# ConvFFN of layer 1 of a diffusion backbone: six up-projection tiles ahead of the norm, H in tiles of its own, eight PSUM banks in turn

## The chip, the cores and the metric

The kernel runs on one core of one Trainium2 chip. The metric is the device time of one execution in microseconds (us). TensorE multiplies matrices into PSUM (eight banks of 512 fp32 columns), ScalarE and VectorE work on SBUF and PSUM, GpSimd on SBUF, and SyncE issues the loads.

## The reference, cut to what matters

Two layers act on 256 latent tokens (and 256 context tokens, which the last layer no longer updates). Behind the token mixer each layer has a gated ConvFFN with a modulated norm in front of it:

```python
def _conv_ffn(h, P):
    u = h @ P['w_up']                                    # 1024 -> 5632
    up = jnp.pad(u, ((0, 0), (1, 1), (0, 0)))
    cw = P['conv_w']
    u = up[:, :-2] * cw[0] + up[:, 1:-1] * cw[1] + up[:, 2:] * cw[2] + P['conv_b']
    g, val = jnp.split(u, 2, axis=-1)
    return (jax.nn.silu(g) * val) @ P['w_down']          # 2816 -> 1024
...
    xl = xl + g1 * y_l
    xl = xl + g2 * _conv_ffn(_rmsnorm(xl, P['norm_ffn']) * (1 + sc2) + sh2, P)
```

All is fp32.

## The kernel before

Features lie on the partitions and tokens on the columns. In layer 1 a tile has 128 features of the 256 latent tokens. To keep fp32's accuracy each product is three matmuls (`mm3`, lines 172 to 174): high part of the weights by high part of the activations, high by low, low by high. `load_w` brings 512 columns of weights (256 KB) into a slot of a ring, lets ScalarE round the high part (line 164) and VectorE or GpSimd subtract the low part (line 168). `lo_on_pool(a, b)` sends a of every b low parts to GpSimd. In the ConvFFN of layer 1 the rings have eight slots in all, so weights can be ready up to four up tiles ahead of TensorE. `unit` makes one output tile of two loads: 8 blocks of rows x 3 matmuls = 24 matmuls.

The ConvFFN has 44 up tiles (called units 0 to 43 here), taken in pairs: `inner(f)` takes units 2f and 2f + 1, lets `conv` apply the three-point convolution to each (ScalarE line 1139, VectorE lines 1142 and 1143), multiplies with the gate (ScalarE 1171, VectorE 1172 and 1173) and splits the product into `ach` (ScalarE 1176) and `acl` (VectorE 1177). These 22 inner tiles are multiplied with the down weights in three groups, of tiles 0 to 7, 8 to 15 and 16 to 21, each with eight output tiles that are added to x (line 1197). The first group comes after inner tile 8, the second and the third after inner tile 21.

In front of it stands the norm: sums of squares on TensorE (line 233), a chain of small VectorE operations that makes the factor (`rsqrt`, lines 197 to 207, and `dg`, line 239), a matmul that spreads it over the partitions (line 242), a copy of it (line 279), and eight steps `hmod`, each of which makes one block of the normed input H: VectorE 265, ScalarE 266, VectorE 267. TensorE does not wait for it in layer 1: while the norm runs, units 0 to 3 are computed ahead from x scaled per feature, which stands in columns 256 to 511 of the `xeh`/`xel` tiles (two columns in front hold the shift, so 258 columns are taken). The factor and the shift are applied to the products afterwards, in `up` (VectorE 1131 and 1132, ScalarE 1133). `run(hsteps, k, UP4)` hands out the norm's ten steps between the blocks k of these units: the sums behind block 1, the spreading behind block 4, the `hmod` steps behind blocks 5 to 7. H is then written into columns 0 to 255 of the same tiles, over the two shift columns, so it follows the reads of units 0 to 3.

The products go to PSUM banks: units 0 to 3 to the four banks of two pair tiles "s" and "t", all later ones in turn to two banks "m" and two banks "o" (`bank`), each of which must have been read by `conv` before it is written again.

The program is written in the order above, and a planner sets each engine's order from it: within an engine it may take a later instruction first when an earlier one isn't ready by its reckoning.

Of the kernel before, what the change touches and what calls it, by code (L numbers as in the profile page):

```python
# [6 lines left out]
F32 = mybir.dt.float32  # L7
F32R = mybir.dt.float32r
# [9 lines left out]
KT = 8  # L18
T = 256
# [13 lines left out]
def hybrid(nc, tc, I, out, dbg=None, stop=None):  # L33
    dbg = dbg or {}
    es = ExitStack()
    mm = nc.tensor.matmul
# [13 lines left out]
    def psum(tag, w=512):  # L50
        return ps.tile([128, 512], F32, tag=tag, name="ps_" + tag, bufs=2)[:, :w]
# [95 lines left out]
    def lo_on_pool(a, b, c=0):  # L147

        lo_mix[:] = [a, b, c]
# [3 lines left out]
    def open_ring(st, name, n):  # L153

        rings.append((st.enter_context(pool(name)), n))
        st.callback(rings.pop)
# [14 lines left out]
    def mm3(o, ah, al, bh, bl, start, stop):  # L171
        mm(o, ah, bh, start=start, stop=False)  # L172
        mm(o, ah, bl, start=False, stop=False)  # L173
        mm(o, al, bh, start=False, stop=stop)  # L174

    def unit(ap, ah, al, w, nk=8, c0=0, p=None, pre=None):
        p = psum("mm", w) if p is None else p
        for k0 in range(0, nk, 4):
            n = min(4, nk - k0)
            hi, lo = pre.pop(0) if pre else load_w(ap[:, 128 * k0:128 * (k0 + n)], 128 * n)  # L180
            for kk in range(n):
                k = k0 + kk
                c = slice(kk * 128, kk * 128 + 128)
                mm3(p, hi[:, c], lo[:, c], ah[k][:, c0:c0 + w], al[k][:, c0:c0 + w], k == 0, k == nk - 1)
        return p
# [98 lines left out]
    def run(steps, i, plan):  # L284

        for _ in range(plan.get(i, 0)):
            if steps:
                steps.pop(0)()


    UNITS = {0: 1, 2: 1, 3: 2, 4: 2, 5: 2, 6: 2}
    UP4 = {1: 1, 4: 1, 5: 3, 6: 3, 7: 2}
    FIRST = {0: 1, 2: 1, 3: 2, 4: 2, 5: 2, 6: 2}
    carried = []

# [21 lines left out]
    def layer(l):  # L317
# [777 lines left out]
        with pool(f"f{l}") as fp, ExitStack() as rst:  # L1095
            nf = (3, 2)[l]
            ps_s, ps_t = pair2("s"), pair2("t")
            p4 = [ps_s[:, 0], ps_s[:, 1], ps_t[:, 0], ps_t[:, 1]]
            for s in range(NS):
                q = slice(T * s, T * s + T)  # L1100
                for k in range(KT):
                    wh, wl = load_w(I["wup4"][l, k], 512)
                    for u in range(4):
                        c = slice(128 * u, 128 * u + 128)
                        if last:
                            mm3(p4[u][:, :T + 2], wh[:, c], wl[:, c], Hh[k][:, T - 2:], Hl[k][:, T - 2:], k == 0, k == KT - 1)
                        else:
                            mm3(p4[u][:, q], wh[:, c], wl[:, c], Hh[k][:, q], Hl[k][:, q], k == 0, k == KT - 1)
                    run(hsteps, k, UP4)
                while hsteps:  # L1110
                    hsteps.pop(0)()
                if s == 0:
                    open_ring(rst, f"ringf{l}", nf)

            lo_on_pool(*((1, 1), (1, 3))[l])

            turn = [0]

            def bank(w):
                turn[0] += 1  # L1120
                t = ("mmst", "mmoo")[l][turn[0] % 4]
                return psum("mm", w) if t == "m" else psum("o", w) if t == "o" else pair2(t)[:, 0, :w]

            def up(i):
                if i >= 4:
                    return unit(I["wup"][l, i], Hh, Hl, W, p=bank(W))
                if not last:
                    return p4[i]
                u = fp.tile([128, T], F32, tag="ue", name="ue", bufs=2)
                cu = small.tile([128, 1], F32, tag="cu", name="cu")  # L1130
                V.tensor_copy(cu, p4[i][:, 0:1])
                V.tensor_tensor(out=u, in0=p4[i][:, 2:T + 2], in1=rb, op=ALU.mult)
                S.activation(u, u, AF.Identity, bias=cu)
                return u

            def conv(p, t):
                y = fp.tile([128, NTOK], F32, tag="cy", name="cy", bufs=4)[:, :W]
                w = [P(l, O_CONVW + 44 * i + t) for i in range(3)]
                S.activation(y, p, AF.Identity, bias=P(l, O_CONVB + t), scale=w[1])
                pv = p.rearrange("p (s t) -> p s t", t=T)  # L1140
                yv = y.rearrange("p (s t) -> p s t", t=T)
                V.scalar_tensor_tensor(out=yv[:, :, 1:], in0=pv[:, :, :T - 1], scalar=w[0], in1=yv[:, :, 1:], op0=ALU.mult, op1=ALU.add)
                V.scalar_tensor_tensor(out=yv[:, :, :T - 1], in0=pv[:, :, 1:], scalar=w[2], in1=yv[:, :, :T - 1], op0=ALU.mult, op1=ALU.add)  # L1143
                return y

            mtodo = {}
            if not last:
                def later(key, l, tiles, both=True):
                    mtodo.setdefault(key, []).extend([lambda t=t: modcol(fp, l, t, both) for t in tiles])
                for i in range(4):  # L1150
                    later(3 + i, 0, range(40 + 2 * i, 42 + 2 * i))
                mtodo[6].append(lambda: modsum(0, 5))
                for j in range(8):
                    later((0, j), 1, [j])
                    later(8 + j, 1, [8 + j])
                    later((1, j), 1, range(16 + 2 * j, 18 + 2 * j), False)
                mtodo[15].append(lambda: (modsum(1, 0), modsum(1, 1), ab(1, 0)))
                for i in range(5):
                    later(16 + i, 1, range(32 + 3 * i, 35 + 3 * i), False)
                later(19, 1, [47], False)  # L1160
                mtodo.setdefault((2, 4), []).append(lambda: ([modsum(1, wh, 1) for wh in (2, 3, 4, 5)], ab(1, 1, False)))

            def todo(key, ins):
                with tc.issue_after(ins):
                    for g in mtodo.pop(key, []):
                        g()
            def inner(f):
                g = conv(up(2 * f), f)
                v = conv(up(2 * f + 1), FT + f)
                th = fp.tile([128, NTOK], F32, tag="th", name="th", bufs=2)[:, :W]  # L1170
                S.activation(th, g, AF.Tanh, scale=0.5)  # L1171
                V.scalar_tensor_tensor(out=g, in0=th, scalar=1.0, in1=g, op0=ALU.add, op1=ALU.mult)
                V.tensor_tensor(out=v, in0=g, in1=v, op=ALU.mult)
                hi = fp.tile([128, W], F32R, tag="ach", name="ach", bufs=nac)
                lo = fp.tile([128, W], F32R, tag="acl", name="acl", bufs=nac)
                S.activation(hi, v, AF.Copy, scale=0.5)  # L1176
                r = V.scalar_tensor_tensor(out=lo, in0=v, scalar=0.5, in1=hi.bitcast(F32), op0=ALU.mult, op1=ALU.subtract)
                todo(f, r.ins)
                ach.append(hi)
                acl.append(lo)  # L1180


            groups = ([[0, 8, 10], [8, 16, 18], [16, 22, 22]], [[0, 8, 9], [8, 16, 22], [16, 22, 22]])[l]
            nac = (11, 22)[l]
            ach, acl = [], []
            for gi, (f0, f1, done) in enumerate(groups):
                while len(ach) < done:
                    inner(len(ach))
                end = gi == len(groups) - 1
                if end and not last:  # L1190
                    lo_on_pool(0, 1)
                for ss in ([[s] for s in range(NS)] if end else [list(range(NS))]):
                    for j in range(KT):
                        p = unit(I["wdn"][l, j][:, 128 * f0:128 * f1], ach[f0:f1], acl[f0:f1], T * len(ss), nk=f1 - f0, c0=T * ss[0], p=bank(T * len(ss)))
                        for i, s in enumerate(ss):
                            c = slice(T * s, T * s + T)
                            r = V.scalar_tensor_tensor(out=x[j][:, c], in0=p[:, T * i:T * i + T], scalar=mcol(l, 5, s, j), in1=x[j][:, c], op0=ALU.mult, op1=ALU.add)
                        todo((gi, j), r.ins)
                        run(hsteps, j, UNITS)
                    if end and not last:  # L1200
                        while hsteps:
                            hsteps.pop(0)()
                        hsteps = norm(1, 0, ss[0])
            carried[:] = hsteps if not last else []
# [143 lines left out]
```

## Time and profile before

| | us |
|---|---|
| median of three runs | 1488.95 (1488.82 to 1491.21) |
| profiled execution, time | 1488.52 |
| its span in the profile | 1486.7 |
| TensorE busy | 1421.6 (96%) |
| VectorE busy | 1205.5 (81%) |
| ScalarE busy | 808.8 (54%) |
| GpSimd busy | 430.5 (29%) |

Times in the rows are microseconds from the span's start. PE is TensorE's matmuls, DVE VectorE, ACT ScalarE, POOL GpSimd. The ConvFFN of layer 1 runs from about 1279 to 1475. Matmuls overlap in the pipeline: the time from one start to the next is their pace, and the duration shown is longer. Some matmul records can be missing. PEclk is the granted clock of TensorE as a share of 2.4 GHz.

### The profile page before, as it was taken

To read this page: it belongs to the slowest core of one execution; us is meant where nothing else is said; L and a number is where in the kernel's file an instruction comes from. 1 tells how busy PE (TensorE), PEld (TensorE's weight loads), DVE (VectorE), ACT (ScalarE), POOL (GpSimd) and SP (SyncE) were. 2 spreads that over 40 slices of the span, in tenths; PEclk is the share of its full clock that TensorE was granted. 3 is DMA by queue.
4 is the path that set the end of the run, shared out by engine and by line. 5 is a ranking of instruction groups with operands and counts; after the bars stand their busy time and mean duration, and the time that the engine had idled before them with its cause. 6 is when DMAs were issued, how large, how long until landed. Compare 5 with 4: busy or idle time off the path is not lost.

```text
span 1486.7 us, 28000 instructions
## 1 busy us (share of the span) xinstructions
PE 1421.6 (96%) x10222; PEld 1241.3 (83%) x10222; DVE 1205.5 (81%) x2316; ACT 808.8 (54%) x1690; POOL 430.5 (29%) x325
## 2 busy tenths in 40 slices
PE   6999989999999999999999999998899899989997
PEld 4787867778788899888888889997788789989997
DVE  4689797878886788898878979979677876997885
ACT  3575455656653356533344235675467666665663
POOL 0001333233320002547544630002244442223331
PEclk9999999999999999999999999999899999999998
DMA  8522132232335576454655865532223336556563
GB/s 312 171 84 67 43 99 90 79 92 89 100 117 176 154 227 207 128 165 144 206 149 160 296 223 149 184 126 69 82 83 94 95 114 191 176 162 198 175 173 92
DMA packets 108650, 213.45 MB, mean 144 GB/s; under 512 B 12128, under 2 KB 21728, under 8 KB 107488
## 3 DMA queue, kind: packets, MB, share of 16 engines
q1 hardware_dynamic: 107824, 211.00, 45.9%
q8 instruction: 81, 1.33, 0.4%
q10 hardware_dynamic: 688, 0.66, 0.1%
q14 instruction: 57, 0.47, 0.1%
HBM read 210.56 MB, written 1.05 MB: 142 GB/s over the span
## 4 chain that ended last, share of the span: by engine, by line
PE 79%; DVE 15%; ACT 3%; issue 3%; DMA 1%; SPq 0%; DVEq 0%; ACTq 0%
PE ps_mm L172 15%; PE ps_mm L174 15%; PE ps_mm L173 15%; PE ps_pair L172 5%; PE ps_pair L174 5%; PE ps_pair L173 5%; PE ps_o L174 2%; PE ps_o L172 2%; PE ps_o L173 2%; PE ps_pair L867 2%; PE ps_pair L905 2%; DVE wlo L168 1%; PE ps_o L924 1%; PE ps_o L921 1%; DVE p L889 1%
## 5 line engine op out<-in xcount | busy, mean ns | idle before, releaser
L168 POOL TENSOR_TENSOR wlo<-raw,whi 128x512 fp32r<-128x512 f32 (+1 forms) x270 | 378.0, 1405 | 833.3 <-ACT whi L164 573.5
L164 ACT CAST whi<-raw 128x512 fp32r<-128x512 f32 (+1 forms) x614 | 360.6, 597 | 301.9 <-PE ps_mm L173 125.5
L172 PE MATMUL ps_mm<-hh,whi 128*128 128x512 f32 (+1 forms) x760 | 275.3, 362 | 3.3 <-DVE qf L997 2.0
L173 PE MATMUL ps_mm<-hl,whi 128*128 128x512 f32 (+1 forms) x760 | 271.8, 358 | 0.0
L174 PE MATMUL ps_mm<-hh,wlo 128*128 128x512 f32 (+1 forms) x760 | 271.1, 357 | 0.0
L168 DVE TENSOR_TENSOR wlo<-raw,whi 128x512 fp32r<-128x512 f32 (+1 forms) x344 | 233.5, 689 | 34.8 <-ACT whi L164 31.8
L172 PEld LDWEIGHTS ps_mm<-hh,whi 128*128 128x128 f32 x760 | 144.5, 190 | 27.4 <-issue 3.2
L174 PEld LDWEIGHTS ps_mm<-hh,wlo 128*128 128x128 f32 x760 | 144.3, 190 | 22.5 <-issue 0.4
L173 PEld LDWEIGHTS ps_mm<-hl,whi 128*128 128x128 f32 x760 | 144.5, 190 | 21.0 <-issue 0.4
L104 DVE SCALAR_TENSOR_TENSOR jk<-wm,sil 128x1024 f32<-128x1024 f32 x96 | 153.3, 1597 | 1.6 <-DMA wm<-wmod 0.6
L172 PE MATMUL ps_pair<-hh,whi 128*128 128x512 f32 (+1 forms) x312 | 109.7, 353 | 0.6 <-ACT whi L164 0.6
L174 PE MATMUL ps_pair<-hh,wlo 128*128 128x512 f32 (+1 forms) x312 | 109.0, 352 | 0.3 <-DVE wlo L168 0.2
L173 PE MATMUL ps_pair<-hl,whi 128*128 128x512 f32 (+1 forms) x312 | 109.2, 351 | 0.0
L909 ACT CAST pth<-ps_pair 128x512 fp32r<-128x512 f32 (+1 forms) x96 | 49.5, 516 | 46.1 <-PE ps_pair L905 29.4
L172 PEld LDWEIGHTS ps_pair<-hh,whi 128*128 128x128 f32 x312 | 58.5, 188 | 9.9 <-ACT whi L164 1.2
L174 PEld LDWEIGHTS ps_pair<-hh,wlo 128*128 128x128 f32 x312 | 58.4, 188 | 9.7 <-DVE wlo L168 0.9
L910 DVE TENSOR_TENSOR ptl<-ps_pair,pth 128x512 fp32r<-128x512 f32 (+1 forms) x96 | 57.3, 597 | 11.0 <-ACT pth L909 10.2
L173 PEld LDWEIGHTS ps_pair<-hl,whi 128*128 128x128 f32 x312 | 58.6, 188 | 8.6
L172 PE MATMUL ps_mm<-ach,whi 128*128 128x256 f32 (+1 forms) x200 | 63.7, 319 | 1.6 <-ACT ach L1176 1.1
L173 PE MATMUL ps_mm<-acl,whi 128*128 128x256 f32 (+1 forms) x200 | 63.5, 317 | 0.0
L174 PE MATMUL ps_mm<-ach,wlo 128*128 128x256 f32 (+1 forms) x200 | 63.4, 317 | 0.0
L1171 ACT ACTIVATE th<-cy 128x512 f32<-128x512 f32 (+1 forms) x44 | 23.0, 523 | 59.8 <-DVE cy L1143 59.6
(684 smaller groups left out, 3687.7 us busy)
## 6 DMA issues: line engine op xcount, KB each, us to landing
raw<-wup SPq DMA_DIRECT2D x184, 256.0 KB, 3.2
raw<-win SPq DMA_DIRECT2D x166, 256.0 KB, 2.8
wm<-wmod SPq DMA_DIRECT2D x64, 512.0 KB, 4.2
raw<-wdn SPq DMA_DIRECT2D x88, 256.0 KB, 3.0
raw<-wbr SPq DMA_DIRECT2D x48, 256.0 KB, 2.7
raw<-wout SPq DMA_DIRECT2D x48, 256.0 KB, 3.0
wm<-wm SPq DMA_DIRECT2D x8, 1024.0 KB, 8.3
wm<-wmod SPq DMA_DIRECT2D x32, 256.0 KB, 2.6
```

The costliest lines, as they stand in the source:

```text
L104: V.scalar_tensor_tensor(out=jk, in0=wm, scalar=1.0, in1=sil[:, s], op0=ALU.mult, op1=ALU.mult, accum_out=MOD[l][:, s, t:t + 1])
L164: S.copy(hi[:, :ncols], raw[:, :ncols])
L168: e.tensor_tensor(out=lo[:, :ncols], in0=raw[:, :ncols], in1=hi[:, :ncols].bitcast(F32), op=ALU.subtract)
L172: mm(o, ah, bh, start=start, stop=False)
L173: mm(o, ah, bl, start=False, stop=False)
L174: mm(o, al, bh, start=False, stop=stop)
L867: mm(sp[:, i, :w], q[:, qc], k[:, kc], start=a == 0, stop=a == n - 1 and not mk)
L889: (G if i < (0, 1)[l] else V).tensor_scalar(out=pts[1 - i], in0=pts[1 - i], scalar1=st_[:, 7 - i:8 - i], scalar2=None, op0=ALU.mult)
L905: nc.tensor.transpose(tp[:, i, c], pts[i][:, c], ident)
L909: S.copy(dh, tv)
L910: V.tensor_tensor(out=dl, in0=tv, in1=dh.bitcast(F32), op=ALU.subtract)
L1171: S.activation(th, g, AF.Tanh, scale=0.5)
```

## The change

Everything is in layer 1's ConvFFN, except that the weight ring is opened one statement earlier in both layers.

- Units 4 and 5 are also computed ahead from the scaled x, into the two banks "m". The norm's spreading step stands behind block 6 in place of 4, three `hmod` steps behind block 7, four behind unit 4 and one behind unit 5.
- H gets sixteen tiles of its own, 256 columns wide (`fhh`, `fhl`).
- The factor and the shift are applied to all six tiles at once, before the first inner tile, into six buffers.
- All later tiles take eight banks in turn: o, o, both halves of s, both halves of t, m, m.
- The low parts of the weights are made on VectorE alone (before: one of three on GpSimd) until inner tile 6, and one of three on GpSimd from there.

```diff
     UP4 = {1: 1, 4: 1, 5: 3, 6: 3, 7: 2}
+    UP4L = {1: 1, 6: 1, 7: 3}
...
+            xeh, xel = list(Hh), list(Hl)
+            if last:
+                for k in range(KT):
+                    Hh[k] = fp.tile([128, T], F32R, name=f"fhh{k}")
+                    Hl[k] = fp.tile([128, T], F32R, name=f"fhl{k}")
...
-                            mm3(p4[u][:, :T + 2], wh[:, c], wl[:, c], Hh[k][:, T - 2:], Hl[k][:, T - 2:], k == 0, k == KT - 1)
+                            mm3(p4[u][:, :T + 2], wh[:, c], wl[:, c], xeh[k][:, T - 2:], xel[k][:, T - 2:], k == 0, k == KT - 1)
...
-                    run(hsteps, k, UP4)
+                    run(hsteps, k, UP4L if last else UP4)
+                if s == 0:
+                    open_ring(rst, f"ringf{l}", nf)
+                if last:
+                    for i in (4, 5):
+                        p4.append(unit(I["wup"][l, i], xeh, xel, T + 2, c0=T - 2, p=psum("mm", T + 2)))
+                        run(hsteps, i, {4: 4})
                 while hsteps:
                     hsteps.pop(0)()
-                if s == 0:
-                    open_ring(rst, f"ringf{l}", nf)
-
-            lo_on_pool(*((1, 1), (1, 3))[l])
+
+            lo_on_pool(*((1, 1), (0, 1))[l])
...
+            half = {}
             def bank(w):
                 turn[0] += 1
-                t = ("mmst", "mmoo")[l][turn[0] % 4]
+                if last:
+
+                    t = "oossttmm"[(turn[0] - 1) % 8]
+                    if t in "st":
+                        if t not in half:
+                            half[t] = pair2(t)
+                            return half[t][:, 0, :w]
+                        return half.pop(t)[:, 1, :w]
+                else:
+                    t = "mmst"[turn[0] % 4]
                 return psum("mm", w) if t == "m" else psum("o", w) if t == "o" else pair2(t)[:, 0, :w]
             def up(i):
-                if i >= 4:
+                if i >= len(p4):
                     return unit(I["wup"][l, i], Hh, Hl, W, p=bank(W))
-                if not last:
-                    return p4[i]
-                u = fp.tile([128, T], F32, tag="ue", name="ue", bufs=2)
+                return p4[i] if not last else us[i]
+
+            def scaled(i):
+                u = fp.tile([128, T], F32, name=f"ue{i}")
                 cu = small.tile([128, 1], F32, tag="cu", name="cu")
                 V.tensor_copy(cu, p4[i][:, 0:1])
                 V.tensor_tensor(out=u, in0=p4[i][:, 2:T + 2], in1=rb, op=ALU.mult)
                 S.activation(u, u, AF.Identity, bias=cu)
                 return u
+            us = [scaled(i) for i in range(len(p4))] if last else []
...
                 while len(ach) < done:
+                    if last and len(ach) == 6:
+                        lo_on_pool(1, 3)
                     inner(len(ach))
```

## Rows read from the trace of the kernel before

**Rows 1.** The page, busy time, share of the span and instructions of each engine.
```profile
PE 1421.6 (96%) x10222; PEld 1241.3 (83%) x10222; DVE 1205.5 (81%) x2316; ACT 808.8 (54%) x1690; POOL 430.5 (29%) x325
```
**Rows 2.** Busy time by stretch: length, then PE, PEld, DVE, ACT, POOL, clock, DMA.
```profile
1290.00:1308.00 18.00, 15.21 (x127) 14.81 (x125) 18.00 (x43) 15.27 (x33) 7.45 (x3) 1.00 0.37 116
1308.00:1314.00 6.00, 5.72 (x36) 5.75 (x37) 4.75 (x14) 3.83 (x9) 0.00 (x0) 0.72 0.12 43
1314.00:1330.00 16.00, 15.15 (x130) 14.82 (x130) 15.97 (x28) 8.93 (x18) 6.38 (x4) 1.00 0.70 213
1330.00:1341.00 11.00, 11.00 (x98) 11.00 (x98) 9.31 (x18) 7.04 (x16) 4.39 (x3) 1.00 0.67 194
1362.00:1434.00 72.00, 71.42 (x623) 70.97 (x621) 60.67 (x111) 44.81 (x93) 22.24 (x16) 1.00 0.60 175
```
**Rows 3.** TensorE in order of time: start, duration, line, tiles; idle before, releaser.
```profile
1278.82 0.29 PE L172 MATMUL ps_pair<-xeh,whi 128*128 128x258 f32 x1
...
1282.52 0.36 PE L172 MATMUL ps_pair<-xeh,whi 128*128 128x258 f32 x1
...
1288.62 0.70 PE L242 MATMUL ps_o<-dg,ones 128*128 128x256 f32 x2 [1.55 <-DVE dg L239]
1288.97 0.47 PE L172 MATMUL ps_pair<-xeh,whi 128*128 128x258 f32 x1
...
1308.28 0.55 PE L172 MATMUL ps_mm<-xeh,whi 128*128 128x256 f32 x1 [3.07 <-ACT ach L1176]
...
1311.62 0.32 PE L172 MATMUL ps_mm<-xeh,whi 128*128 128x256 f32 x1
...
1361.68 0.29 PE L172 MATMUL ps_o<-xeh,whi 128*128 128x256 f32 x1
...
1434.49 0.36 PE L172 MATMUL ps_mm<-ach,whi 128*128 128x256 f32 x1 [0.54 <-DVE cy L1143]
```
**Rows 4.** VectorE in order of time.
```profile
1295.39 0.41 DVE L1132 TENSOR_TENSOR ue<-ps_pair,x 128x256 f32<-128x256 f32 x1
...
1298.21 0.68 DVE L168 TENSOR_TENSOR wlo<-raw,whi 128x512 fp32r<-128x512 f32 x1
1298.81 0.47 DVE L1143 SCALAR_TENSOR_TENSOR cy<-ue,pp,cy 128x255 f32<-128x255 f32 x1
1299.21 1.52 DVE L1142 SCALAR_TENSOR_TENSOR cy<-ue,pp,cy 128x255 f32<-128x255 f32 x1
...
1303.78 1.51 DVE L1143 SCALAR_TENSOR_TENSOR cy<-ue,pp,cy 128x255 f32<-128x255 f32 x1
...
1315.21 1.52 DVE L1177 SCALAR_TENSOR_TENSOR acl<-cy,ach 128x256 fp32r<-128x256 f32 x1
...
1340.65 0.42 DVE L1177 SCALAR_TENSOR_TENSOR acl<-cy,ach 128x256 fp32r<-128x256 f32 x1 [0.48 <-ACT ach L1176]
```
**Rows 5.** GpSimd in order of time.
```profile
1283.37 1.65 POOL L168 TENSOR_TENSOR wlo<-raw,whi 128x512 fp32r<-128x512 f32 x1 [35.20 <-ACT whi L164]
...
1302.83 2.18 POOL L168 TENSOR_TENSOR wlo<-raw,whi 128x512 fp32r<-128x512 f32 x1 [2.38 <-ACT whi L164]
1314.83 3.06 POOL L168 TENSOR_TENSOR wlo<-raw,whi 128x512 fp32r<-128x512 f32 x2 [9.83 <-ACT whi L164]
```
**Rows 6.** TensorE in order of time: first matmuls of runs with one moving tile.
```profile
1241.88 0.28 PE L172 MATMUL ps_mm<-ybh,whi 128*128 128x256 f32 x1
...
1243.30 0.29 PE L172 MATMUL ps_mm<-hh,whi 128*128 128x256 f32 x1
...
1369.86 0.28 PE L172 MATMUL ps_o<-xeh,whi 128*128 128x256 f32 x1
...
1375.30 0.28 PE L172 MATMUL ps_mm<-xeh,whi 128*128 128x256 f32 x1
...
1443.19 0.28 PE L172 MATMUL ps_mm<-ach,whi 128*128 128x256 f32 x1
...
1448.95 0.28 PE L172 MATMUL ps_o<-ach,whi 128*128 128x256 f32 x1
```

## The prediction

> **What bounds the kernel now.** I read the page first: TensorE is busy for 96% of the span [rows 1], so a gain must come from a stretch in which TensorE waits or runs slowly. The table by stage then shows where that is. Through most of layer 1's ConvFFN (1362 to 1434 us) TensorE is busy 71.4 of 72 us. Only the opening, 1290 to 1314, shows a hole; and there VectorE is busy 18.00 of 18 us, then 4.75 of 6, 15.97 of 16 and 9.31 of 11 [rows 2]. So in the opening two engines are near their limit, and VectorE is idle only 1.25 + 0.03 + 1.69 = 3.0 of 51 us. TensorE's list in order of time names the holes [rows 3]: 1.55 us until the norm's factor (dg) is ready, 3.07 us at 1308.28 until a PSUM bank is evacuated (the row names ach; unit 8 needs unit 4's bank, whose last reader, on VectorE, ended at about that time), and then a granted clock of 0.72 over 1308 to 1314 [rows 2], that is 1.2 GHz for part of it: sixteen matmuls from 1308.28 to 1311.62 take 3.34 us, at the later pace 1.8, so 1.5 us lost. The last wait in this stretch is therefore VectorE's, and the question is whether the change takes work from VectorE or only lets TensorE run ahead of it.
>
> **What VectorE spends.** A low part costs it 0.60 us (1298.21 to 1298.81 [rows 4]). A low part on GpSimd is not free for it: operations that take 0.47 or 0.42 us take 1.52, 1.51 and 1.52 at 1299.21, 1303.78 and 1315.21, just while GpSimd runs a low part (for example 1302.83, 2.18 us) [rows 4, 5]. Each of those held VectorE by about 1.05 us, more than the work itself.
>
> **The pace of a matmul.** With H, which lies in the left half of tiles of 512 columns, 48 matmuls of 256 columns take 1375.30 - 1369.86 = 5.44 us, 0.1133 each. With the FFN's own inner tiles as moving operand, 48 take 1448.95 - 1443.19 = 5.76, 0.1200 each; with the attention's output yb, 12 take 1.42, 0.118 each [rows 6], all at a granted clock of 1.00. Weights, ring and banks are of the same kinds, so the moving tile makes the difference; why, the rows don't tell. The change gives H tiles of its own, 256 columns wide, like every tile that shows 0.118 to 0.120. I take 0.120, and keep 0.1133 for the range.
>
> The Trainium skill (TensorE: Matmul & The Clock Gate, Back-to-back issue gap) gives the gap from the number of columns alone, N / 2.4 + 2.5 ns, 109 ns for 256; by it H's new place would cost nothing, and the sum below would end near 1486.4 in place of 1490.5. The two paces above are at odds with it.
>
> **TensorE alone, by the rows.** From the first matmul of the tiles ahead (1278.82) to the end of the first down group (1361.68) it took 82.9 us [rows 3]. After the change, with no wait: six tiles ahead, 144 matmuls of 258 columns x 0.12 = 17.3; the norm's small matmuls 0.8 + 0.35 = 1.2 (24 matmuls and the first of these fill the 3.70 from 1278.82 to 1282.52, and the second runs from 1288.62 to 1288.97); units 6 to 17, 12 x 24 x 0.12 = 34.6; eight down tiles, 8 x 24 x 0.12 = 23.0. Sum 76.1, 6.8 less. From 1361.68 to 1434.49 it took 72.8 for 26 up tiles, bank waits included (0.54 is the last, 1434.49). After: 26 x 24 x 0.12 = 74.9, 2.1 more, though eight banks take those waits away. Behind that only the inner tiles are read, at the pace of before. The two columns more of units 4 and 5 are inside the 0.12. TensorE alone would end 4.7 us earlier.
>
> **Whether VectorE lets it.** The first down tile needs the eighth inner tile. Before, its low half (acl) ran from 1340.65 to 1341.07 [rows 4]; TensorE came to it at 1361.68 - 7 x 2.88 - 3 x 0.12 = 1341.2, with 0.1 us of slack. After, TensorE by itself would be there 6.8 us earlier, at 1334.4. VectorE's sum up to that acl changes so:
> - The factor's matmul moves behind k = 6: 1282.52 + 60 x 0.12 = 1289.7 in place of 1288.6 [rows 3], so H starts 1.1 later (the 1.55 us wait itself goes). +1.1.
> - Two more scaled tiles, a copy and a product each, 0.4 together (the product 0.41, 1295.39 [rows 4]): +0.8. ScalarE gets two more Identity operations; it is busy 15.3 of 18 us there [rows 2], so I let them hide.
> - Six low parts of units 4 to 11 come from GpSimd; the first two (from 1283.37 on [rows 5]) fall into time that VectorE has to spare before the factor is due, four count: +4 x 0.60 = +2.4. The stalls that go with them go too, the three named: -3.2. One further low part can now be made before H starts: -0.6.
> - Of VectorE's idle 3.0 us, the 1.25 in 1308 to 1314 came from the slow TensorE: -1.25. The rest is ScalarE's turn within a chain, and stays.
> Net -0.75: the acl is there at about 1340.3, and TensorE, ready at 1334.4, waits 6 us somewhere before it. Bounds: -4 if all idle time is recovered and no low part comes before its turn; +2.3 if nothing is recovered and three further low parts (1.8) stand ahead.
>
> A wait of 3.07 us was followed by the 1.5 us of 1.2 GHz, the one of 1.55 was not [rows 3]. Six microseconds in one piece would cost 1.5, in small pieces nothing: I take 0.75.
>
> H's own tiles save a wait of the norm's writes for the matmuls that still read the old ones; nothing waited for that before, since the steps ran behind them: 0, and needed only because six tiles are ahead. The scaled tiles with buffers of their own: 0 by themselves. Eight banks in turn: they take a wait away only where VectorE follows in time. The loads are the same in number and size.
>
> **The sum.** Opening: -0.75 + 0.75 = 0. Units 18 to 43: +2.1. Bank waits there are inside it. The profiled execution took 1488.52 us (span 1486.7), so 1490.6, say 1490.5; the median of the runs shown, 1488.95, lies 0.4 above it, within their scatter. The change removes what TensorE waits for, not what VectorE has to do, and the gain is handed back there.
>
> **Rivals.**
> 1. *TensorE really gets ahead* (0.22). VectorE isn't held by GpSimd in the first twelve units, fills its waits, and the eighth inner tile is there by 1335.5. For it: 3.2 us of stalls do go. Against it: VectorE would have to do its 48 busy us of this stretch 5 us sooner. -4.7 + 0.7 for small waits: 1484.5.
> 2. *The pace of H does not change* (0.12). Opening 0, units 18 to 43 at 0.1133: 70.7, -2.1: 1486.4. Against it the tiles of rows 6. Both 1 and 2 (0.05): 12 x 24 x 0.0067 = 1.9 more in the opening and 4.2 more behind: 1478.
> 3. *Low parts come behind the inner chains* (0.20), the other side. In program order scaled tiles and three inner tiles now stand ahead of unit 6's weights. VectorE: H until 1290.9 + 16 x 0.4 = 1297.3, scaled 2.5, three inner tiles of seven operations, 8, to 1307.8, then unit 7's low part, 1308.4. TensorE is there at 1291.5 + 3.5 x 2.88 = 1301.6 and waits 6.8 us in one piece, then 10.5 units x 2.88 + 1.5 at the lower clock: the first down tile begins at 1340.1 against 1338.6, +1.5, and +2.1 behind. With ScalarE's casts late in the same way (up to 1.5): 1492 to 1494. It decides from a wait of about 5.5 us on with the lower clock behind it. For it: at 1308.28 TensorE waited behind the same chains.
> 4. *The turn of banks does not do what it says* (0.03): two of eight banks are halves of one pair tile. If the write of a second half waits for the first half's readers, two of eight tiles wait 1.5 us, 15 of 62: 23 us, 1512.
> The likeliest, as summed, has 0.38; its own range is 1487.5 to 1493.5.
>
> **How the numbers follow.** A measurement of this kernel can tell about 0.2%, 3 us, from no change: 1486.0 to 1491.9 is "same". Faster: rivals 1 and both, and a little of 2: 0.29. Slower: most of 3, 4, and the upper end of the likeliest: 0.27. Same: 0.44. The range goes from 1482 (rival 1 with 2.5 us to spare) to 1494.5 (rival 3's upper end); outside are 4, both of 1 and 2, and tails.
>
> **What would show it.** Right: TensorE no longer waits for dg; a wait or waits of 5 to 7 us in all before the eighth inner tile, with VectorE busy through them; no operation of VectorE of 1.5 us between 1290 and 1315; up tiles of the middle at 2.88 us each instead of 2.72; the first down tile within 1.5 us of 1338.6. Wrong: up tiles still at 2.72 (rival 2), or the first down tile before 1335 (rival 1), or one wait of over 6 us before unit 8 (rival 3).

## The result and the profile after

The changed kernel takes 1501.82 us (median of 4 runs, 1498.29 to 1503.45) beside 1490.08 for the kernel before on the same chip: a ratio of 1.0071, interval 1.0055 to 1.0087. It is 0.7% slower, about 10.6 us by the ratio and 11.7 by the medians. The forecast was 1490.5 in a range from 1482 to 1494.5; the time lies above that range.

In the profiled execution TensorE's busy time rises by 9.4 us against [rows 1], for the same 10222 matmuls; the page's line of busy time, share of the span and instructions:
```profile
PE 1431.0 (95%) x10222; PEld 1249.3 (83%) x10222; DVE 1195.8 (80%) x2325; ACT 811.3 (54%) x1692; POOL 417.0 (28%) x320
```
To say where the time went, I measure one stretch in every trace: from the first matmul that sums the squares of the norm (it stands among the tiles ahead) to the first of the final norm. Before it lasts from 1281.70 to 1474.87, 193.17 us; after from 1284.92 to 1489.80, 204.88. That is 11.7 us more, so all of the difference lies inside layer 1's ConvFFN. Four of the stretches of [rows 2], now in the changed kernel:
```profile
1290.00:1308.00 18.00, 16.42 (x133) 15.96 (x132) 15.80 (x45) 15.01 (x33) 0.00 (x0) 1.00 0.23 72
1308.00:1314.00 6.00, 1.12 (x10) 0.92 (x8) 5.66 (x16) 4.03 (x10) 0.00 (x0) 0.69 0.17 46
1314.00:1330.00 16.00, 15.48 (x107) 15.48 (x108) 12.29 (x25) 7.76 (x16) 4.75 (x3) 0.80 0.64 214
...
1362.00:1434.00 72.00, 69.90 (x577) 69.31 (x577) 53.38 (x105) 44.47 (x88) 22.56 (x16) 1.00 0.57 172
```
Two things are new. From 1308 to 1314 TensorE stands nearly still (1.12 of 6 us) while VectorE works. And in the middle, where TensorE was busy 71.42 of 72 us, it is busy 69.90, and gets through 577 recorded matmuls in place of 623. TensorE's waits from 1252 to 1495 by what was waited for (total, times, longest):
```profile
PE ps_pair L174 <- DVE wlo L168: 5.4, 1, 5.4
PE ps_pair L172 <- DVE cy L1165: 3.1, 4, 1.5
PE ps_o L242 <- DVE dg L239: 2.3, 1, 2.3
PE ps_pair L172 <- ACT whi L164: 0.9, 1, 0.9
PE ps_o L233 <- DVE sq L221: 0.7, 1, 0.7
PE ps_pair L172 <- DVE x L1221: 0.7, 1, 0.7
PE ps_o L174 <- DVE wlo L168: 0.7, 1, 0.7
```
The norm's factor (dg) is no longer waited for in the opening; the one wait of 2.3 us for it is the final norm's, as before. In its place stand 7.0 us for weights: a low part 5.4 and 0.7, a cast 0.9. New too are 3.8 us for readers of a *pair* tile: the convolution (cy, line 1165) and the last x update. In order of time, TensorE:
```profile
1306.51 0.39 PE L172 MATMUL ps_pair<-fhh,whi 128*128 128x256 f32 x1 [0.92 <-ACT whi L164]
...
1307.67 0.38 PE L174 MATMUL ps_o<-fhh,wlo 128*128 128x256 f32 x1 [0.65 <-DVE wlo L168]
...
1314.52 0.58 PE L174 MATMUL ps_pair<-fhh,wlo 128*128 128x256 f32 x1 [5.40 <-DVE wlo L168]
1314.90 0.41 PE L172 MATMUL ps_pair<-fhh,whi 128*128 128x256 f32 x1
1315.12 0.41 PE L173 MATMUL ps_pair<-fhl,whi 128*128 128x256 f32 x1
...
1381.04 0.28 PE L172 MATMUL ps_o<-fhh,whi 128*128 128x256 f32 x1
...
1386.80 0.28 PE L172 MATMUL ps_pair<-fhh,whi 128*128 128x256 f32 x1
```
After the 5.40-us wait the matmuls start 0.21 to 0.22 us apart (1314.90 to 1315.12) until 1320.45. That is the lower clock of 1.2 GHz; the granted clock over 1314 to 1330 is 0.80 as a mean. The stretch from 1314.52 to 1320.45 takes 5.93 us for some 28 matmuls, which at 0.12 take 3.3, so 2.6 us are lost. From 1381.04 to 1386.80, 48 matmuls on H take 5.76 us, 0.1200 each, where [rows 6] show 0.1133. VectorE ahead of that wait:
```profile
1294.34 1.27 DVE L265 SCALAR_TENSOR_TENSOR ht<-x,ab 128x256 f32<-128x256 f32 x3
...
1306.93 0.68 DVE L168 TENSOR_TENSOR wlo<-raw,whi 128x512 fp32r<-128x512 f32 x1
1307.53 0.41 DVE L1199 SCALAR_TENSOR_TENSOR acl<-cy,ach 128x256 fp32r<-128x256 f32 x1
...
1313.45 0.42 DVE L1194 SCALAR_TENSOR_TENSOR cy<-th,cy 128x256 f32<-128x256 f32 x1
1313.78 0.68 DVE L168 TENSOR_TENSOR wlo<-raw,whi 128x512 fp32r<-128x512 f32 x1
```
From 1294.34, where H begins, to 1313.78 it makes one low part. The rest is H, six scaled tiles and the inner chains, with one idle spell of 0.34 us. ScalarE waited 0.95 us for a load that landed at 1311.7, and that spell is all that VectorE lost by it.

### The profile page after: what moved, and what is told of

Its sections match the earlier page's. It is cut to its first block, busy times and chain, and to the rows that moved or that the text cites. A ratio compares the mean times of both kernels' runs of the same rounds, so it can differ in the third digit from the quotient of the medians.

```text
span 1501.1 us, 27929 instructions
## 1 busy us (share of the span) xinstructions
PE 1431.0 (95%) x10222; PEld 1249.3 (83%) x10222; DVE 1195.8 (80%) x2325; ACT 811.3 (54%) x1692; POOL 417.0 (28%) x320
## 4 chain that ended last, share of the span: by engine, by line
PE 78%; DVE 15%; ACT 3%; issue 3%; DMA 1%; SPq 0%; DVEq 0%; ACTq 0%
PE ps_mm L172 15%; PE ps_mm L173 14%; PE ps_mm L174 14%; PE ps_pair L172 7%; PE ps_pair L174 6%; PE ps_pair L173 6%; PE ps_pair L868 2%; PE ps_pair L906 2%; DVE wlo L168 2%; PE ps_o L174 1%; PE ps_o L172 1%; PE ps_o L925 1%; PE ps_o L173 1%; PE ps_o L922 1%; DVE p L890 1%
## 5 line engine op out<-in xcount | busy, mean ns | idle before, releaser
L168 POOL TENSOR_TENSOR wlo<-raw,whi 128x512 fp32r<-128x512 f32 (+1 forms) x265 | 364.9, 1382 | 858.2 <-ACT whi L164 606.7
L172 PE MATMUL ps_pair<-ach,whi 128*128 128x256 f32 (+1 forms) x200 | 63.9, 320 | 0.7 <-DVE x L1221 0.7
L174 PE MATMUL ps_pair<-ach,wlo 128*128 128x256 f32 (+1 forms) x200 | 63.5, 317 | 0.0
L173 PE MATMUL ps_pair<-acl,whi 128*128 128x256 f32 (+1 forms) x200 | 63.4, 317 | 0.0
L172 PE MATMUL ps_mm<-mh,whi 128*128 128x256 f32 x192 | 54.7, 285 | 0.0
```

The source lines that it names most:

```text
L168: e.tensor_tensor(out=lo[:, :ncols], in0=raw[:, :ncols], in1=hi[:, :ncols].bitcast(F32), op=ALU.subtract)
```

## The experiments

Theory 1 (near the forecast's rival 3): the opening ends when VectorE has done its work there, and the low parts come behind the inner chains. Theory 2 (the forecast's rival 4): a matmul into the second half of a pair tile waits for the readers of the first half. Theory 3: H at its new place is read more slowly. "Stretch" is the one defined above; all times in us. Each ratio is to the kernel before on the same chip. The last four rows all have six banks and H early.

| kernel | median | ratio to before, interval | stretch |
|---|---|---|---|
| before | 1489.9 to 1490.9 | 1 | 193.17 |
| changed | 1501.82 | 1.0071 [1.0055, 1.0087] | 204.88 |
| six banks | 1493.91 | 1.0022 [1.0009, 1.0035] | 197.35 |
| halves four units apart | 1494.27 | 1.0027 [1.0016, 1.0038] | 197.02 |
| before, with eight banks | 1497.30 | 1.0052 [1.0032, 1.0071] | 200.57 |
| a third on GpSimd | 1503.06 | 1.0082 [1.0062, 1.0102] | 202.33 |
| scaled tiles one by one | 1505.37 | 1.0090 [1.0069, 1.0111] | 205.86 |
| weights of 6 to 9 first | 1501.22 | 1.0072 [1.0052, 1.0092] | 202.88 |
| six banks, low parts left out | 1487.84 | 0.9982 [0.9971, 0.9994] | 188.51 |
| six banks, four tiles ahead | 1492.22 | 1.0007 [0.9994, 1.0021] | 195.58 |
| changed, 64 bytes | 1501.31 | 1.0074 [1.0057, 1.0091] | 202.46 |
| before, 64 bytes | 1488.92 | 0.9987 [0.9976, 0.9998] | 191.83 |
| before, own tiles of H | 1492.53 | 1.0015 [1.0003, 1.0028] | 194.96 |
| six banks, 64 bytes | 1486.67 | 0.9975 [0.9960, 0.9990] | 190.99 |
| the same, four tiles ahead | 1485.55 | 0.9959 [0.9942, 0.9976] | 186.64 |
| six banks, 64 bytes, H early | 1484.88 | 0.9961 [0.9948, 0.9975] | 187.12 |
| with 128 bytes | 1490.41 | 0.9999 [0.9987, 1.0010] | 193.85 |
| with 32 bytes | 1484.82 | 0.9963 [0.9947, 0.9979] | 191.15 |
| 64, a third on GpSimd | 1482.36 | 0.9959 [0.9944, 0.9975] | 186.78 |
| 64, larger ring | 1484.38 | 0.9952 [0.9935, 0.9968] | 184.40 |

The medians and the stretches can differ by some 4 us; the work ahead of the stretch, which the edits of this section do not touch, ended between 1280.55 and 1290.69 in these profiled executions. Where they differ, the stretch says more about the edit. It is read from one execution per kernel, but parts of it repeat closely: the 26 units behind the first down group took 74.88 us in all five kernels with H in its own tiles and neither unused bytes nor a wait there, and 70.72 in all five with six banks and 64 bytes.

**The halves of a pair tile**

Six banks, each pair tile used by its first half alone:
```diff
-                    t = "oossttmm"[(turn[0] - 1) % 8]
...
+                    t = "oostmm"[(turn[0] - 1) % 6]
```


> The turn uses only the first half of each pair tile, six banks in place of eight. Theory 2: the waits for VectorE's convolution at line 1165 and for the last x update, 3.8 us together, go, and units run in program order again: 3 to 5 us under the changed kernel; if the broken order is also what brought the 5.4-us wait, 9 to 11 us. Theory 1: the waits for low parts in the opening stay at 5 to 8 us, and the time is no more than 4 us lower. Theory 3: within 1 us.


The median is 1493.91, 7.9 under the changed kernel; the stretch is 7.5 shorter. TensorE's waits from 1290 to the end of the stretch:
```profile
PE ps_pair L174 <- DVE wlo L168: 5.4, 1, 5.4
PE ps_mm L172 <- ACT whi L164: 0.7, 1, 0.7
PE ps_o L174 <- DVE wlo L168: 0.7, 1, 0.7
```
Every wait for a reader is gone. The 5.4-us wait stands, so the broken order did not bring it. Theory 2 is worth more than the 3 to 5 us expected of it.

Eight banks, but with the two halves of a pair four units apart:
```diff
-                    t = "oossttmm"[(turn[0] - 1) % 8]
+                    t = "ostmostm"[(turn[0] - 1) % 8]
```


> The changed kernel with the eight banks in another turn, so that the two halves of a pair tile come four units apart in place of one behind the other. Theory 2 (a second half waits for the readers of the first): by then the first half has long been read, so the waits for the convolution and the x update (3.8 us) go without giving up a bank: 1493 to 1496, as with six banks. Rival (six banks was faster because two banks fewer hold the units back less, or by the order of something else): within 2 us of the changed kernel, 1500 to 1503.


The median is 1494.27 and the stretch 197.02: as with six banks. TensorE's waits from 1290 on:
```profile
PE ps_pair L172 <- DVE cy L1165: 4.1, 1, 4.1
PE ps_o L172 <- ACT whi L164: 0.7, 1, 0.7
PE ps_pair L174 <- DVE wlo L168: 0.7, 1, 0.7
```
Behind the opening there is no wait. So the number of banks does nothing here, and the neighbourhood of the halves does it. But the wait of 4.1 us, which ends at 1312.03 in the opening, again names the reader of a pair tile: where VectorE is that far behind, four units between the halves are not enough. It added little, since a low part that TensorE needed there, too, was made only from 1312.13 on.

The kernel before, with the turn of the changed kernel and nothing else:
```diff
-                t = ("mmst", "mmoo")[l][turn[0] % 4]
...
+                    t = "oossttmm"[(turn[0] - 1) % 8]
...
```


> The kernel before with nothing but the turn over eight banks, the halves of a pair tile one behind the other. Theory 2: the second halves wait for the first halves' readers, 6 to 9 us over the kernel before, less the 1.1 us of waits for a bank that it had: 1495 to 1499. Rival (the turn only hurts together with the late low parts of the changed kernel): within 2 us of the kernel before.


The median is 1497.30, the stretch 7.4 longer. Its waits name the convolution that reads a pair, and it needs no late low part for them (from 1265 to 1476):
```profile
PE ps_pair L172 <- DVE cy L1152: 5.8, 5, 1.7
PE ps_o L172 <- ACT ach L1185: 1.9, 1, 1.9
```
Put in alone, the turn over neighbouring halves costs 7.4 us; taken out alone, it gives 7.5.

**The opening**

One low part in three on GpSimd from the start, as before:
```diff
-            lo_on_pool(*((1, 1), (0, 1))[l])
+            lo_on_pool(*((1, 1), (1, 3))[l])
...
-                    if last and len(ach) == 6:
-                        lo_on_pool(1, 3)
```


> Theory 1 (the low parts of the weights come late because VectorE has them behind the scaled tiles and the inner chains): with one low part in three on GpSimd again from the start, GpSimd, which is idle until 1318 in the changed kernel, makes some of them at once; TensorE's waits of 7.0 us for low parts between 1306 and 1315 fall below 3 and the clock stays up; 4 to 8 us under the changed kernel, less what GpSimd's holds of VectorE (1.5 us each before) take back. Theory 2 (the second half of a pair tile waits for the readers of its first half): the bank turn is as in the changed kernel, so within 1.5 us of it. Theory 3 (only the slower pace of the matmuls that read H counts): within 1 us of the changed kernel.


The waits for low parts fall from 6.1 to 1.6, and the stretch by 2.6, but the waits for the convolution of a pair grow from 3.1 to 4.5, and the median (1503.06) shows no gain. Not the 4 to 8 us of theory 1.

The scaled tiles one by one, ahead of their inner chains:
```diff
-                return p4[i] if not last else us[i]
+                return p4[i] if not last else scaled(i)
...
-            us = [scaled(i) for i in range(len(p4))] if last else []
```


> The six scaled tiles are asked for one by one ahead of their inner chains, as before, and not all six up front. Theory 1: up to 3 us of scaled tiles leave the place ahead of the first low parts, so the waits for low parts shrink by 2 to 4 us and the clock falls less: 2 to 6 us under the changed kernel. Rival to it: the inner chains alone fill VectorE and the low parts still come behind them: within 1.5 us. Theories 2 and 3: within 1 us.


The median is 1505.37 and the stretch 205.86: no gain, and the waits for weights are 6.1 us in four pieces.

The weights of units 6 to 9 asked for ahead of the scaled tiles:
```diff
...
+            early = {i: [load_w(I["wup"][l, i][:, 512 * h:512 * h + 512], 512) for h in range(2)] for i in (6, 7, 8, 9)} if last else {}
             us = [scaled(i) for i in range(len(p4))] if last else []
```


> The weights of units 6 to 9 are asked for, and so their low parts placed, ahead of the scaled tiles and the inner chains. Theory 1: the 7.0 us of waits for low parts between 1306 and 1315 fall to 2 or less and the low clock behind them (some 2.6 us) goes: 6 to 10 us under the changed kernel, near the kernel before; what is late next is a bank that the delayed chains still hold, up to 3 us. Theory 2: within 2 us of the changed kernel, as the pairs keep their order. Theory 3: within 1 us.


The median is 1501.22, no gain (6 to 10 us were expected). TensorE's waits from 1290 on show the exchange:
```profile
PE ps_pair L172 <- ACT ach L1199: 4.4, 1, 4.4
PE ps_pair L172 <- DVE cy L1166: 3.5, 4, 1.5
PE ps_mm L174 <- POOL wlo L168: 1.7, 1, 1.7
```
The low parts are there, and now the delayed chains hold the bank (4.4). With this, theory 1 as I had it falls: the order of low parts and chains on VectorE does not matter. What may still bind is the sum of its work, and that I tested by taking work out, with six banks:
```diff
+        if nolo[0]:
+            return hi, hi
...
+                nolo[0] = last and 6 <= i < 12
```


> Six banks, and the low parts of units 6 to 11 are left out (their matmuls read the high part in that place, so TensorE and ScalarE do the same work and VectorE 12 low parts of 0.6 us less). Theory 1 (VectorE's work between the first piece of H and the eighth inner tile sets the opening's end): the waits for low parts, 6.8 us in the run of six banks, fall below 2 and the low clock with them, 5 to 8 us under that run (1493.9). Rival (the chains of the inner tiles or ScalarE's casts bind on their own): waits of 4 us or more for a cast or a bank appear, and the gain is under 3 us.


This kernel leaves out twelve low parts, and the stretch is 8.8 shorter (the median 6.1). TensorE does not wait once from 1290 to 1473, and it runs through the opening at full clock (length, then PE, PEld, DVE, ACT, POOL, clock, DMA):
```profile
1308.00:1314.00 6.00, 6.00 (x52) 6.00 (x51) 6.00 (x16) 5.95 (x14) 1.05 (x1) 1.00 0.47 156
1314.00:1320.00 6.00, 6.00 (x52) 6.00 (x51) 6.00 (x15) 5.38 (x13) 0.75 (x2) 1.00 0.31 108
```
Leaving a low part out also takes away the wait that names it; but the kernel with the weights first shows that a bank or a chain then binds if VectorE's work stays, and here none does. VectorE's sum of work sets the end of the opening.

Four tiles ahead in place of six, with six banks:
```diff
-                    run(hsteps, k, UP4L if last else UP4)
+                    run(hsteps, k, UP4)
...
-                    for i in (4, 5):
+                    for i in ():
```


> Six banks, but only four tiles ahead of the norm as before; H in its own tiles and the low parts on VectorE as in the changed kernel. Theory 1 (VectorE has too much in the opening): with two scaled tiles fewer ahead but the wait for the norm's factor back, the opening's waits are 6 to 9 us as with six tiles: within 2 us of the run of six banks with six tiles (1494). If six tiles ahead are what TensorE gains by: 2 to 5 us slower than that run. If they are what fills VectorE: 2 to 5 us faster.


The median is 1492.22, the stretch 1.8 shorter than with six tiles: waits of 3.4 us in place of 6.8. Two tiles more ahead bring nothing here. With the 64 bytes (below) it is the same question again:


> Six banks, the 64 bytes, and four tiles ahead as in the kernel before. As a sum of the runs so far: 1492.2 with four tiles and six banks, less the 7.2 us that the 64 bytes gave with six tiles: 1484 to 1487. If six tiles are worth anything once the pace is the faster one: 1487 to 1490.


The median is 1485.55 and the stretch 186.64, 4.4 shorter than with six tiles. But this edit also spreads the norm's factor behind k = 4. With six tiles, and only that:
```diff
-                    run(hsteps, k, UP4L if last else UP4)
+                    run(hsteps, k, UP4)
```


> Six banks and the 64 bytes as in an earlier run (1486.7), with six tiles ahead, but the norm's factor is spread behind k = 4 as in the kernel before and not behind k = 6. Theory 1, sharpened: VectorE is idle for some 3 of 12 us while the tiles ahead run and full from the first piece of H on, so everything behind moves with H's start, 24 matmuls of 0.12 = 2.9 us earlier if the factor is there: the 5.8-us wait shrinks by 2 to 3 us and the time is 2 to 3.5 us under that run, 1483 to 1485. Rival (the weights' casts and loads set the opening's end): within 1 us of it.


The median is 1484.88, the stretch 3.9 shorter; the longest wait falls from 5.8 to 3.0. First with six banks and 64 bytes, then with H early:
```profile
PE ps_pair L174 <- DVE wlo L168: 5.8, 1, 5.8
```
```profile
PE ps_o L174 <- DVE wlo L168: 3.4, 2, 3.0
```
The ratios (0.9975 and 0.9961) overlap, so this rests on the stretch. By it, H's late start is what six tiles cost, and with H early six or four tiles are alike.

The low parts' engine once more, without the pair trouble (the edit of the first kernel of this group, on the last one):


> The best version so far (six banks, 64 bytes, H early: 1484.9) with one low part in three on GpSimd from the start, as in the kernel before. If the move to VectorE is what fills VectorE in the opening: the 3.0-us wait goes and the time is 2 to 4 us under that version. If GpSimd's holds of VectorE (1.5-us operations) take back what it does: within 1.5 us, with such operations to be seen again. If GpSimd's slow low parts are themselves late: 1 to 4 us over it, with a wait that names GpSimd.


The stretch is 186.78 against 187.12: nothing. VectorE pays as it did in [rows 4, 5]; first VectorE, then GpSimd in order of time:
```profile
1308.41 1.52 DVE L1161 SCALAR_TENSOR_TENSOR cy<-ue,pp,cy 128x255 f32<-128x255 f32 x1
1309.86 1.76 DVE L168 TENSOR_TENSOR wlo<-raw,whi 128x512 fp32r<-128x512 f32 x1
```
```profile
1308.38 2.69 POOL L168 TENSOR_TENSOR wlo<-raw,whi 128x512 fp32r<-128x512 f32 x2 [12.29 <-ACT whi L164]
```
An operation of 0.47 takes 1.52, a low part 1.76 in place of 0.68, while GpSimd makes its two. The Trainium skill (SBUF — State Buffer, Who interferes with whom) says that these two engines share a pair of ports as an exclusive lock; these rows agree.

More room for weights in layer 1, on the version with H early:
```diff
-            nf = (3, 2)[l]
+            nf = (3, 4)[l]
```


> The same version with four more places for weights in layer 1 in place of two, so that low parts can be made while VectorE is idle ahead of H. Theory 1: VectorE's 3 idle us between 1284 and 1296 take up to four low parts of 0.6; the 3.0-us wait shrinks by 2 us or more, the time is 1.5 to 3.5 us under that version. If the loads come no sooner, or the places fill up with weights whose turn is later: within 1 us of it.


The stretch is 184.40, 2.7 shorter; TensorE's waits from 1290 on:
```profile
PE ps_o L172 <- ACT ach L1195: 1.3, 1, 1.3
PE ps_o L172 <- DVE cy L1162: 0.6, 1, 0.6
PE ps_pair L174 <- DVE wlo L168: 0.2, 1, 0.2
```
2.2 us are left of the 4.4 that the same version had. The ratios (0.9952 and 0.9961) overlap, so in the total this is not settled. It has the shortest stretch of all, 8.8 under before, and its ratio is 0.5% under before.

**The pace on H**

In the compiled kernels, the old tiles of H start 64 bytes after a multiple of 128 in each partition, the new ones and the down projection's operands at a multiple of 128. So I moved the latter two by 64 unused bytes; 64 more ahead of the ring keep the weights at a multiple of 128:
```diff
+                fp.tile([128, 16], F32, name="pad")
...
+                        rings[-1][0].tile([128, 16], F32, name="pad2")
```


> The changed kernel with 64 unused bytes ahead of the new tiles of H and of the down projection's operands, which moves all of these by 64 bytes in the on-chip memory; the order of TensorE's work stays as it is. Theory 3 (the pace of a matmul of 256 columns hangs on where its moving tile lies, 0.1133 us at the old place of H, 0.1200 at the new one): the up units fall to 0.1133 a matmul, 38 units of 24 by 0.0067 = 6.1 us, and the down projection too, 528 matmuls by 0.0067 = 3.5 us: 9 to 10 us under the changed kernel. Rival (the slower pace comes from the bank turn or from the second copy of H itself): 0.1200 stays, within 1 us of the changed kernel.


The median does not move (1501.31) where 9 to 10 us were expected; the stretch is 2.4 shorter. The pace did change (units between 0.1133 and 0.118), but TensorE then met the readers of the pairs sooner: 5.2 us for cy in place of 3.1. Faster matmuls were in part paid back at the next wait.


> The kernel before with the same 64 unused bytes, which move only the down projection's operands and the scaled tiles; H lies where it was. Theory 3: the down projection's matmuls fall from 0.1200 to 0.1133, 528 by 0.0067 = 3.5 us: 2.5 to 4 us under the kernel before. Rival: the pace stays, within 1 us of it.


In the kernel before, where H stays, the ratio is 0.9987 and the stretch 1.3 shorter; the down tiles run at 0.1133 to 0.118. Less than expected.

Six banks and the 64 bytes:


> Six banks as in the run of six banks, and the 64 bytes as well. Theories 2 and 3 together, as a sum: 8 us under the changed kernel by the banks and 9 to 10 us by the place, 1483 to 1486, so 5 to 8 us under the kernel before. If the place does nothing: 1493 to 1495.


The median is 1486.67, a little above the 1483 to 1486 expected, and the stretch is 6.4 under that of six banks. 48 matmuls on H from 1372.48 to 1377.92 are 5.44 us, 0.1133 each, again as in [rows 6]:
```profile
1372.48 0.28 PE L172 MATMUL ps_mm<-fhh,whi 128*128 128x256 f32 x1
...
1377.92 0.28 PE L172 MATMUL ps_o<-fhh,whi 128*128 128x256 f32 x1
```
With 128 and with 32 bytes, H early:


> The same version with 128 unused bytes in place of 64, so that H and the down projection's operands start at a multiple of 128 bytes again. If the place within 128 bytes sets the pace: 0.1200 a matmul again, 6 to 8 us over that version, 1491 to 1493. If any shift helped: 0.1133 and within 1.5 us of it.

> The same version with 32 unused bytes. No theory tells this one beforehand: if only 64 within 128 gives the pace, 0.1200 and 1491 to 1493; if every start off a multiple of 128 bytes does, 0.1133 and 1483 to 1486.5; between them a pace of its own.


The 26 units behind the first down group take 0.1189 a matmul with 128 bytes, and the stretch is 6.7 longer than with 64; with 32 bytes they take 0.1169, and it is 4.0 longer. So the place does it and not any shift, but 128 bytes do not give back 0.1200 quite, and the median with 32 bytes (1484.82) shows nothing of the longer stretch. The place is not all either: in the kernel before, the units on H at its old place mix 0.1133 and 0.118. Which rule joins place and pace stays open.

H in its own tiles, in the kernel before:
```diff
+                    Hh[k] = fp.tile([128, T], F32R, name=f"fhh{k}")
+                    Hl[k] = fp.tile([128, T], F32R, name=f"fhl{k}")
```


> The kernel before with nothing but tiles of its own for H (at a multiple of 128 bytes); the order of TensorE's work stays that of before. Theory 3: the up units go at 0.1200 in place of 0.1133 to 0.118, 26 units by 24 by 0.0060 = 3.7 us behind the opening and up to 1.3 in it: 3 to 5 us over the kernel before. Rival: the pace of H follows from the later VectorE or the banks, within 1 us of it.


The median is 1492.53, the stretch 1.8 longer. The 26 units behind the first down group begin and end here:
```profile
1361.88 0.28 PE L172 MATMUL ps_o<-fhh,whi 128*128 128x256 f32 x1
...
1436.76 0.28 PE L172 MATMUL ps_mm<-ach,whi 128*128 128x256 f32 x1
```
They take 74.88 us in place of the 72.81 of [rows 3], and the waits for the norm's factor and for the last two banks, 2.6 us before, are gone. Less than the 3 to 5 us expected.

## Why the prediction was wrong

The steps of the sum against the run of six banks, which is the changed kernel without the pair trouble, and then that trouble:

| step | forecast | measured | from |
|---|---|---|---|
| opening, first matmul ahead to first down tile | 0 | +2.15 | 59.84 (1278.82 to 1338.66) before, 61.99 (1285.32 to 1347.31) with six banks |
| first down group | 0 | 0.0 | 23.02 and 23.04 |
| units 18 to 43 | +2.1 | +2.07 | 72.81 and 74.88 |
| behind them | 0 | -0.1 | 40.38 and 40.32 |
| pair halves | 0 | +7.5 | 204.88 - 197.35 |
| sum | +2.1 | +11.7 | |

**The step that failed** is the sum's term for the turn over eight banks. The sum put it at nothing, on the sentence that eight banks take the bank waits away; the runs show 7.5 us, the larger part of the loss. The cause stood in rival 4, "the turn of banks does not do what it says", and I gave it 0.03. There the mechanism was named rightly: the second half's write waits for the first half's readers. Its price was wrong: 23 us, since I let fifteen second halves wait 1.5 each; the trace has five waits of 0.3 to 1.5 behind the opening. In the kernel TensorE's order puts other units between the halves. Of the 7.5 us, these five waits are 3.8 and their edges 0.8; the low clock behind the opening's wait, as long in both, cost 2.6 in place of 1.4, which no edit explains, so that some 6.3 us are the halves' own; the opening's own waits are 0.2 longer. The last 1.5 are late starts too short for the list of waits: 0.07 at the second matmul behind each of the five waits, and some 0.14 at each of eight more switches to a pair tile, as here, where 0.12 would be the pace:
```profile
1374.53 0.28 PE L173 MATMUL ps_mm<-fhl,whi 128*128 128x256 f32 x1
1374.73 0.36 PE L172 MATMUL ps_pair<-fhh,whi 128*128 128x256 f32 x1
1374.93 0.28 PE L173 MATMUL ps_pair<-fhl,whi 128*128 128x256 f32 x1
```
Behind the opening, six banks show none of these. So nothing of the 7.5 is left for the changed order of units by itself. A row could have warned me: with four banks TensorE already met the convolution at a bank's turn ([rows 3], 0.54), and a second half's turn comes sooner after its neighbour's unit than any of those.

**The opening** came out as rival 3. I had TensorE 6.8 us earlier and waiting 6, with 0.75 for the clock: 0. With six banks the waits are 6.8, their edges 0.5, the low clock 1.4: 8.7, less the 6.8 that TensorE comes earlier, is 1.9 of the 2.15 measured. That rival's long wait (6.8) and its condition (about 5.5 us in one piece) nearly held: 5.4 in one piece, with the low clock behind it; its sign, one wait of over 6, did not show. The reason I gave was half right: VectorE's whole work decides, not the place of the low parts in it. And the +1.1 for the later spreading of the factor was the term to look at: undoing it, with the steps of H that follow, gave 3.9 of the stretch.

**Right** were the wait for dg that goes, the middle tiles at 2.88 in place of 2.72, the absence of 1.5-us operations on VectorE, and the middle's +2.1 to within 0.1. That the new tiles would be read at 0.1200 was partly luck: I argued from their width of 256 columns, and the same tiles 64 bytes further on are read at 0.1133. Rival 2 is out: its condition fails at 0.1200. Its sum was off, too: it took 0.1133 for all of the middle before, where units at 0.118 are among them, so that with the old pace and no bank wait it would have saved some 1.6 us and not 2.1 (71.2, as an estimate from a mean of 0.1141, in place of 72.81). The Trainium skill (TensorE: Matmul & The Clock Gate, Back-to-back issue gap) gives the isolated gap of a matmul from its columns alone; for 256 columns that is 109 ns, as an estimate from its formula, which the forecast set against a stream of matmuls. The runs show 0.1133, 0.1169, 0.1189 and 0.1200 us for 256 columns, by the place of the moving tile, so the measurement decides. Rival 1 had its cause in view: without VectorE's low parts TensorE does run ahead, by 8.8 us, but the move from GpSimd does not free VectorE.

## What to carry to other kernels

In these kernels a bank was not a buffer of its own where two of them are halves of one tile: before turning over both, look which reader the second half's first write waits for, or put other units between the halves, more of them where the reader lags. Running one engine further ahead helps only if the engine behind it starts no later; here the steps moved behind the tiles ahead cost 3.9 us of the stretch. And a gain in pace may in part be paid back at the next wait (2.4 of the stretch and nothing of the total, against 6.4 once the waits were gone), so remove the wait first, then measure the rest.

## What the runs showed of the hardware that was not expected

The same 256-column matmul took 0.1133, 0.1169 and 0.1189 us on the mean with its moving tile shifted by 64, 32 and 128 bytes, and 0.1200 unshifted. A wait of 5.4 us was followed by some 28 matmuls at 1.2 GHz in the changed kernel and by 13 with six banks (1318.08 to 1321.02): the same wait, two prices. And the work ahead of the ConvFFN ended up to 10 us earlier or later from one profiled execution to another, more than most of these edits are worth.
